# The end of a row-wise maximum kernel: who waits for the last store, and where the closing barriers stand

## The chip, the cores and the metric

The kernel runs on one core of one Trainium2 chip. The metric is the device time of one execution in microseconds (us), lower is better. Before the change it was 628.59 us (median of 3 runs, 628.57 to 628.78).

## The reference

```python
def setup_inputs():
    return {"x": np.random.randn(8192, 8192).astype(np.float32)}

def reference(x):
    return np.linalg.norm(x, ord=np.inf, axis=1)   # the largest |x| of each row
```

The kernel reads 268.44 MB and writes 8192 numbers.

## The kernel before

SyncE issues all loads, VectorE reduces each tile with an absolute maximum, and the results leave in three small stores. The last store, 128 numbers of four bytes, is issued by SyncE and waits for the last reduction.

```python
    for a in range(A):
        for n in range(G):
            t = sbuf.tile([P, W + PAD], F32, tag="t")          # three buffers
            nc.sync.dma_start(out=t[:, :W], in_=x_b[a, n])
            absmax(r_bulk[:, a, n * B : (n + 1) * B], ...)
    nc.scalar.dma_start(out=out_b, in_=r_bulk[:])
    # ... the last 16 rows of each partition in smaller and smaller loads ...
                    absmax(r_fin[:], t[:, lo : W + n_last - 1])  # the last reduction
    nc.sync.dma_start(out=out_t[:, n_tail - 1 :], in_=r_fin[:])  # the last store
    nc.at_finalize(start_first_load_early)                       # moves the first load ahead
```

Nothing in this source says how the program ends. The framework writes that: a last block of instructions in which, in this order,

1. SyncE waits for all eight DMA semaphores (100 to 107) and for VectorE's (99), in four two-semaphore waits and one drain;
2. all five engines meet in barrier one (each of the four others counts up semaphore 96, GpSimd waits for the four counts and then releases them through semaphore 97);
3. GpSimd drains and clears semaphores 99 to 107 with one range clear;
4. all five engines meet in barrier two, built like the first.

Of the kernel before, what the change touches and what calls it, by code (L numbers as in the profile page):

```python
# [1 line left out]
logging.getLogger("concourse").setLevel(logging.ERROR)  # L3

# [1 line left out]

# [4 lines left out]

F32 = mybir.dt.float32
X = mybir.AxisListType.X



TAIL = [
    [2944, 13440],
    [4096, 12288],
    [11520, 4864],  # L20
    [7680, 8704],
    [6528, 3328, 6528],
    [4864, 4096, 3328, 4096],
    [3968, 3584, 3328, 2944, 2560],
    [2432, 2176, 1920, 1664, 1536, 1280, 1152, 1024, 1152, 1024, 1024],
]


def segments(loads, cols):

    out, at = [], 0
    for i, w in enumerate(loads):
        end = at + w
        while at < end:
            r = at // cols
            to = min(end, (r + 1) * cols)
            out.append((i, r, at - r * cols, to - at))
            at = to
    return out


def start_first_load_early(nc):


    sp = mybir.EngineType.SP
    first, *rest = nc.main_func.blocks
    for block in rest:
        insts = block.instructions
        for i, ins in enumerate(insts):
            if ins.engine == sp and type(ins).__name__ == "InstDMACopy":  # L50
                assert not ins.sync_info.on_wait
                moved = insts[i]
                block.instructions = insts[:i] + insts[i + 1 :]
                head = first.instructions
                at = next(k for k, h in enumerate(head) if h.engine == sp)
                first.instructions = head[:at] + [moved] + head[at:]
                return


@with_exitstack  # L60
def kernel(
    ctx: ExitStack,
    tc: tile.TileContext,
    x: bass.AP,
    out: bass.AP,
    G: int = 4,
    B: int = 2,
    BUFS: int = 3,
    PAD: int = 16,
):  # L70
    nc = tc.nc
    P = nc.NUM_PARTITIONS
    rows, cols = x.shape
    W = B * cols


    n_tail = B * len(TAIL)
    n_bulk_rows = rows // P - n_tail
    assert n_bulk_rows % (G * B) == 0
    A = n_bulk_rows // (G * B)  # L80
    split = n_bulk_rows * P
    x_b = x[:split].rearrange("(a p n b) c -> a n p (b c)", p=P, a=A, n=G, b=B)
    out_b = out[:split].rearrange("(a p n b) -> p a (n b)", p=P, a=A, n=G, b=B)
    x_t = x[split:].rearrange("(p t b) c -> t p (b c)", p=P, b=B)
    out_t = out[split:].rearrange("(p t) -> p t", p=P)

    sbuf = ctx.enter_context(tc.tile_pool(name="sbuf", bufs=BUFS))
    outp = ctx.enter_context(tc.tile_pool(name="outp", bufs=1))

    segs = [segments(loads, cols) for loads in TAIL]  # L90
    count = {}
    for i, s in enumerate(segs):
        for _, r, _, _ in s:
            count[i * B + r] = count.get(i * B + r, 0) + 1
    n_last = count[n_tail - 1]
    k_max = max(count[r] for r in range(n_tail - 1))
    assert n_last - 1 <= PAD

    r_bulk = outp.tile([P, A, G * B], F32)
    r_tail = outp.tile([P, n_tail], F32)  # L100
    r_fin = outp.tile([P, 1], F32)
    part = outp.tile([P, n_tail - 1, k_max], F32)
    nc.vector.memset(part[:], 0.0)  # L103

    def absmax(o, i):
        nc.vector.reduce_max(out=o, in_=i, axis=X, apply_absolute_value=True)  # L106

    for a in range(A):
        for n in range(G):
            t = sbuf.tile([P, W + PAD], F32, tag="t")  # L110
            nc.sync.dma_start(out=t[:, :W], in_=x_b[a, n])
            absmax(
                r_bulk[:, a, n * B : (n + 1) * B],
                t[:, :W].rearrange("p (b c) -> p b c", b=B),
            )
    nc.scalar.dma_start(out=out_b, in_=r_bulk[:])

    seen = {}
    for i, loads in enumerate(TAIL):
        t = sbuf.tile([P, W + PAD], F32, tag="t")  # L120
        todo = segs[i]
        at = 0
        for j, w in enumerate(loads):
            nc.sync.dma_start(out=t[:, at : at + w], in_=x_t[i][:, at : at + w])  # L124
            at += w
            for _, b, c, n in [s for s in todo if s[0] == j]:
                r = i * B + b
                k = seen.get(r, 0)
                seen[r] = k + 1
                lo = b * cols + c  # L130
                if r < n_tail - 1:
                    absmax(part[:, r, k : k + 1], t[:, lo : lo + n])
                    if r == n_tail - 2 and k == count[r] - 1:

                        absmax(r_tail[:, : n_tail - 1], part[:])
                        nc.scalar.dma_start(
                            out=out_t[:, : n_tail - 1], in_=r_tail[:, : n_tail - 1]
                        )
                elif k < n_last - 1:
                    absmax(t[:, W + k : W + k + 1], t[:, lo : lo + n])  # L140
                else:

                    absmax(r_fin[:], t[:, lo : W + n_last - 1])
    nc.sync.dma_start(out=out_t[:, n_tail - 1 :], in_=r_fin[:])
    nc.at_finalize(start_first_load_early)


# [1 line left out]
_INS = ['x']  # L149
_OUTS = [((8192,), 'float32')]  # L150


# [23 lines left out]
```

## Time and profile before

The page of the profiled run before (span, busy share of the DMA engines in 40 slices, chain that ended last):

```profile
span 627.3 us, 201 instructions
...
DMA  9999999999999999999999999999999999999997
...
HBM read 268.44 MB, written 0.03 MB: 428 GB/s over the span
## 4 chain that ended last, share of the span: by engine, by line
DMA 67%; DVE 28%; another core or an unknown queue 4%; SPq 0%; issue 0%
```

The DMA engines are busy 90% or more in every slice but the last: the kernel is a read from memory at 428 GB/s. Nothing in the last block can change that; it can only change what happens after the reading. The timeline of the last two instructions (start, duration, engine, line, operation):

```profile
623.80 1.23 DVE L106 TENSOR_REDUCE r_fin<-t 128x1 f32<-128x1030 f32 x1
625.05 0.35 SPq L144 DMA_DIRECT2D out_dram<-r_fin  x1
```

The view of SyncE's waits (who waited for whom: total us, times, longest), and the DMA view's line of the last store (size of one, us from issue to landing):

```profile
SPq L171 <- DMA out_dram<-r_fin: 0.9, 1, 0.9
SPq L171 <- PEq L171: 0.6, 2, 0.4
```

```profile
out_dram<-r_fin SPq DMA_DIRECT2D x1, 0.5 KB, 1.4
```

L171 stands for the framework's last block. SyncE sits 0.9 us in an end wait for the last store, which takes 1.4 us to land; while it waits, the four other engines wait for it in barrier one. The view of one source line shows the block's instructions (count: duration in ns, least/median/most; first and last start):

```profile
L171 SPq EVENT_SEMAPHORE  x6: 17/28/898, 625.5 to 627.3; - x6
L171 POOLq EVENT_SEMAPHORE  x4: 17/17/17, 626.7 to 627.2; - x4
...
L171 POOLq EVENT_SEMAPHORE_RANGE_CLEAR  x1: 92/92/92, 626.9 to 626.9; - x1
```

SyncE has six semaphore instructions (four end waits, two in barriers), one of 898 ns; GpSimd's four belong to the two barriers and the first of them starts at 626.7, that is, after the landing.

The packed trace's own records of semaphores and instructions give this to the nanosecond (the views round to 0.1 us). Times are from the span's start:

```
625.024  VectorE   last reduction ends
625.052  SyncE     last store issued
625.587  SyncE     wait on semaphores 106 and 101, lasts 898 ns
626.463            sixteenth and last landing of the store on semaphore 101
626.485  SyncE     that wait ends
626.677  GpSimd    barrier one: all four counts seen
626.935  GpSimd    range clear, 92 ns
627.213  GpSimd    barrier two: release (17 ns), its last instruction
627.317  TensorE   out of barrier two: end of the span
627.552 627.586 627.791 627.835 627.858 627.957 627.996 628.030 628.077   semaphore 2 counted
628.863 ... 629.218                                                       counted nine times more
```

Semaphore 2 is not the kernel's. It belongs to what the runtime runs after the kernel, and that is inside the measured time: this run was timed at 629.09 us, and its last count of semaphore 2 is at 629.218.

### The profile page before, as it was taken

What the parts mean: (1) busy time and instruction counts of PE and PEld (TensorE: products, weight loads), DVE (VectorE), ACT (ScalarE), POOL (GpSimd) and SP (SyncE); (2) the same over time, 40 slices, a digit from 0 to 9 for tenths busy, and PEclk for the clock granted to TensorE, in tenths of its full rate; (3) what the DMA queues carried; (4) which work ended last, traced back from release to release, by engine and by line L of the source; (5) the groups of instructions that cost most, each with busy time, mean ns of one, the idle gap of its engine ahead of it and who ended that gap; (6) DMA issues with size and microseconds to landing.
All of it is one profiled execution on the core that took longest, in us unless ns stands there. A gap on an engine that the chain in (4) does not pass through costs nothing.

```text
span 627.3 us, 201 instructions
## 1 busy us (share of the span) xinstructions
DVE 553.0 (88%) x64; POOL 0.2 (0%) x4
## 2 busy tenths in 40 slices
DVE  0688998888988889888898888998889999999998
POOL 0000000000000000000000000000000000000000
DMA  9999999999999999999999999999999999999997
GB/s 401 468 401 468 401 468 401 464 405 455 414 451 418 451 418 401 468 401 468 401 468 401 468 401 468 401 468 401 468 418 406 460 430 410 436 422 430 428 423 287
DMA packets 8994, 268.49 MB, mean 428 GB/s; under 512 B 1952, under 2 KB 1952, under 8 KB 3104
## 3 DMA queue, kind: packets, MB, share of 16 engines
q1 hardware_dynamic: 8064, 268.44, 99.3%
q10 hardware_dynamic: 928, 0.03, 0.1%
q14 instruction: 2, 0.02, 0.0%
HBM read 268.44 MB, written 0.03 MB: 428 GB/s over the span
## 4 chain that ended last, share of the span: by engine, by line
DMA 67%; DVE 28%; another core or an unknown queue 4%; SPq 0%; issue 0%
DMA t<-in_x_dram 67%; DVE r_bulk L106 22%; DVE part L106 5%; DVE t L106 1%; DVE r_fin L106 0%; SPq L124 0%; DVE r_tail L106 0%
## 5 line engine op out<-in xcount | busy, mean ns | idle before, releaser
L106 DVE TENSOR_REDUCE r_bulk<-t 128x2 f32<-128x16384 f32 x24 | 413.3, 17220 | 70.1 <-DMA t<-in_x_dram 70.1
L106 DVE TENSOR_REDUCE part<-t 128x1 f32<-128x8192 f32 (+18 forms) x31 | 130.5, 4273 | 0.9 <-DMA t<-in_x_dram 0.6
L106 DVE TENSOR_REDUCE t<-t 128x1 f32<-128x1152 f32 (+3 forms) x6 | 7.9, 1387 | 0.0
L106 DVE TENSOR_REDUCE r_fin<-t 128x1 f32<-128x1030 f32 x1 | 1.2, 1226 | 0.0
L103 DVE MEMSET part<- 128x60 f32 x1 | 0.1, 108 | 0.9 <-PEq L160 0.9
L106 DVE TENSOR_REDUCE r_tail<-part 128x15 f32<-128x60 f32 x1 | 0.2, 216 | 0.0
L160 POOL MEMSET const-bfloat16-1.0<- 128x1 bf16 x1 | 0.1, 103 | 0.0
L160 POOL MEMSET const-uint8-127<- 128x1 uint8 x1 | 0.1, 103 | 0.0
L160 POOL MEMSET const-float32-1.0<- 128x1 f32 x1 | 0.1, 100 | 0.0
L160 POOL MEMSET const-float32-0.0<- 128x1 f32 x1 | 0.1, 99 | 0.2 <-issue 0.2
## 6 DMA issues: line engine op xcount, KB each, us to landing
t<-in_x_dram SPq DMA_DIRECT2D x1, 6720.0 KB, 40.4
t<-in_x_dram SPq DMA_DIRECT2D x2, 3264.0 KB, 26.4
t<-in_x_dram SPq DMA_DIRECT2D x3, 2048.0 KB, 29.0
t<-in_x_dram SPq DMA_DIRECT2D x1, 6144.0 KB, 40.6
t<-in_x_dram SPq DMA_DIRECT2D x1, 5760.0 KB, 35.3
t<-in_x_dram SPq DMA_DIRECT2D x3, 1664.0 KB, 32.5
t<-in_x_dram SPq DMA_DIRECT2D x2, 2432.0 KB, 32.6
t<-in_x_dram SPq DMA_DIRECT2D x1, 4352.0 KB, 42.8
```

The source lines that it names most:

```text
L103: nc.vector.memset(part[:], 0.0)
L106: nc.vector.reduce_max(out=o, in_=i, axis=X, apply_absolute_value=True)
L160: nc = _bacc.Bacc("TRN2", target_bir_lowering=False, num_devices=1)
```

## The change

The intent is that the closing barriers need not wait for the last store. After the change SyncE makes no end waits; the barriers start as soon as it has issued the store. GpSimd alone waits for all DMAs, behind both barriers, and then clears the semaphores. Since the program ends there, no engine should need a barrier behind the clear. That is argued.

```diff
+def finish_on_pool(nc):
+    sp, pool = mybir.EngineType.SP, mybir.EngineType.Pool
+    body, end = nc.main_func.blocks[-2:]
+    # ... finds the last store's semaphore (lane), SyncE's end wait (src),
+    # ... and GpSimd's drain and range clear (drain, clear) in the last block (insts) ...
+    waits = sorted(src.sync_info.on_wait, key=lambda s: s.id == lane)   # the last store's lane last
+    wait = mybir.InstDrain(
+        name=nc.get_next_instruction_name(),
+        engine=pool, ins=[], outs=[],
+        sync_info=mybir.SyncInfo(on_wait=waits, on_update=[]),
+    )
+    moved = {src.name, drain.name, clear.name}
+    end.instructions = [i for i in insts if i.name not in moved] + [wait, clear]
 ...
     nc.at_finalize(start_first_load_early)
+    nc.at_finalize(finish_on_pool)
```

More of the change, by code (lines that the diff above doesn't have):

```diff
@@ L57, in start_first_load_early @@
                 return
+def finish_on_pool(nc):
+    sp, pool = mybir.EngineType.SP, mybir.EngineType.Pool
+    body, end = nc.main_func.blocks[-2:]
+    last_store = [
+        i
+        for i in body.instructions
+        if i.engine == sp and type(i).__name__ == "InstDMACopy"
+    ][-1]
+    lane = last_store.sync_info.on_update[0].id
+    insts = end.instructions
+    src = next(i for i in insts if i.engine == sp)
+    assert type(src).__name__ == "InstDrain" and not src.sync_info.on_update
+    at = next(k for k, i in enumerate(insts) if type(i).__name__ == "InstISA")
+    drain, clear = insts[at - 1], insts[at]
+    assert drain.engine == clear.engine == pool
+    assert type(drain).__name__ == "InstDrain"
+    assert not (drain.sync_info and drain.sync_info.on_wait)
+    waits = sorted(src.sync_info.on_wait, key=lambda s: s.id == lane)
+    assert waits[-1].id == lane
+    wait = mybir.InstDrain(
+        name=nc.get_next_instruction_name(),
+        engine=pool,
+        ins=[],
+        outs=[],
+        sync_info=mybir.SyncInfo(on_wait=waits, on_update=[]),
+    )
+    moved = {src.name, drain.name, clear.name}
+    end.instructions = [i for i in insts if i.name not in moved] + [wait, clear]
 @with_exitstack
```

## The prediction

> **What bounds the kernel now.** A read of 268.44 MB: the page's DMA row is 9 in 39 of 40 slices, mean 428 GB/s, and the chain of waits is 67% DMA. The change touches none of that; every load, reduction and store keeps its order. It touches only what follows the last store, so I read the end of the span (timeline, and the trace's records of semaphores). Times are us from the span's start:
>
> - 625.02: the last reduction ends. 625.05 to 625.40: SyncE issues the last store.
> - 625.45: SyncE begins four end waits. The third, for the last store's lane, is held until 626.485; the sixteenth landing came at 626.463 (DMA view: 1.4 us from issue to landing).
> - 626.52 to 626.65: SyncE's fourth wait, its drain, its arrival at barrier one.
> - 626.68 to 626.86: barrier one. 626.84 to 627.03: GpSimd's drain and its range clear (92 ns). To 627.317: barrier two, end of the span.
>
> So 0.85 us follow the landing in series, and for 1.0 us before it the engines only wait.
>
> **What the change does.** Both barriers start when SyncE has issued the store, about 625.45, while it is in flight. Estimates from the steps above: barrier one 0.2 us, barrier two without the clear 0.3, so both are over near 626.0. Then GpSimd does three waits already satisfied, 78 ns each (its spacing of two semaphore instructions), to about 626.25: still before the landing, which I leave at 626.46. So the barriers are wholly hidden. Behind the landing remain: wake 22 ns, step to the drain 40, drain 34 to 70, step 30, clear 92: about 0.24 us instead of 0.85. The span should end at about 626.70, 0.61 us earlier; every engine but GpSimd is done near 626.0.
>
> **How much of it counts.** The time measured, 628.59, exceeds the span, 627.3: something after the kernel's instructions counts too. The Trainium skill, Runtime: NRT & Kernel Launch, "The ~15µs preamble/postamble breakdown", names a barrier and a reset of 51 semaphores per engine there. This trace agrees that they exist: semaphore 2 counts from 627.55 to 628.08, and nearly all others are reset by 628.64. In that barrier the third arrival is late: 205 ns after the second, against 38 ns at the same place in the barrier before the kernel. I take it for GpSimd, 0.56 us after its last instruction at 627.23. If it keeps that distance from its new last instruction (626.72), it arrives at 627.28, 0.51 us earlier, and the rest shifts with it. The gain is 0.5 to 0.6 us, nearly all on the critical path, but under 0.1% of the whole.
>
> **Predicted time: 628.05 us**, 628.59 less 0.54, range 627.7 to 628.4. Faster by over 2%: 0.5%; within 2%: 99%; slower by over 2%: 0.5%.
>
> **What would show each step right or wrong.** Both barriers' records between 625.4 and 626.1 on all engines; no end wait of SyncE; one long GpSimd wait ending some 20 ns after the last landing; drain and clear last, the clear ending at 626.65 to 626.75; landing still 1.4 us after issue; loads and reductions within 0.1 us of before; the semaphore-2 count resumed about 0.5 us earlier.
>
> **What would make it wrong.** The loads' time, 622 us, drifting by a few tenths between runs or chips, which could hide or double the gain. GpSimd's three satisfied waits running past the landing. The after-kernel part hanging on an engine other than GpSimd, or having a fixed wait of its own. The clear, now last, costing more than its record tells.

## The result, and the profile after

The changed kernel took 628.01 us (median of 6 runs, 627.88 to 628.20) against 628.63 us before in the same rounds (628.43 to 629.10). The two groups of runs do not overlap. The ratio, which is the mean time of the fast runs of one kernel over that of the other's of the same rounds and so not quite the ratio of the medians, is 0.9989 with a 95% interval of 0.9976 to 1.0002. By that interval alone the gain would not be certain; the trace has to decide. Of the experiments below, only runs 6, 9 and 10 have an interval wholly below 1, and at a threshold of 2% every kernel here counts as the same.

The page after:

```profile
span 626.0 us, 199 instructions
...
DMA  9999999999999999999999999999999999999997
...
HBM read 268.44 MB, written 0.03 MB: 429 GB/s over the span
## 4 chain that ended last, share of the span: by engine, by line
DMA 67%; DVE 29%; another core or an unknown queue 4%; SPq 0%; issue 0%
```

The bulk is the same. The timeline's last two lines after:

```profile
623.11 1.23 DVE L139 TENSOR_REDUCE r_fin<-t 128x1 f32<-128x1030 f32 x1
624.37 0.35 SPq L177 DMA_DIRECT2D out_dram<-r_fin  x1
```

Here is a trap. The span is 1.3 us shorter, but the last reduction already starts 0.69 us earlier (623.11 against 623.80), although the change does nothing before it. The profiled run before was among the slowest of its group (629.09 us), the one after the fastest of its own (627.88 us). So 0.68 us of the difference of the two profiles lies before the end of the last reduction, where no instruction was changed: I call it drift of the loads. From here on I count from the end of the last reduction, and call the time from there to the last count of semaphore 2 the **tail**. It is 4.194 us before and 3.662 us after: **0.532 us** is what the change gained.

The view of SyncE's waits after, the DMA view's line of the last store, and the views of the two source lines that the last block's instructions now carry:

```profile
SPq L205 <- PEq L205: 0.4, 2, 0.3
```

```profile
out_dram<-r_fin SPq DMA_DIRECT2D x1, 0.5 KB, 1.4
```

```profile
L205 POOLq EVENT_SEMAPHORE  x4: 17/17/17, 624.9 to 625.3; - x4
...
L205 SPq EVENT_SEMAPHORE  x2: 17/17/17, 625.0 to 625.4; - x2
...
L205 POOLq EVENT_SEMAPHORE_RANGE_CLEAR  x1: 92/92/92, 626.0 to 626.0; - x1
```

```profile
bacc.py:44 POOLq EVENT_SEMAPHORE  x4: 42/42/43, 625.4 to 625.8; - x4
```

SyncE's wait for the store is gone from its list. The four barrier instructions of GpSimd are at 624.9 to 625.3, before the landing (625.78), where they were behind it. The four new end waits are GpSimd's (the line of bacc.py:44). The store takes 1.4 us as before. In the trace's records, from the end of the last reduction:

```
                                         before    after
last store issued                         0.028    0.027
barrier two over on GpSimd                2.206    1.004
third satisfied end wait over               -      1.303
last landing of the store                 1.439    1.440
clear ends                                2.003    1.706
end of the span                           2.293    1.706
semaphore 2, 1st count                    2.528    1.326
             2nd count                    2.562    1.360
             3rd count                    2.767    2.233
             9th count                    3.053    2.518
            18th count (tail)             4.194    3.662
```

The first two counts come 1.2 us earlier, and then the count stands still for 0.87 us until the third. So the third engine in the runtime's barrier is the one that everybody waits for. That it is GpSimd, the engine that finishes last, is still an inference here; runs 6, 7, 9 and 11 test it.

### The profile page after: what moved, and what is told of

Read it like the earlier page. It is cut to its first block, busy times and chain, and to the rows that moved or that the text cites. A ratio compares the mean times of both kernels' runs of the same rounds, so it can differ in the third digit from the quotient of the medians.

```text
span 626.0 us, 199 instructions
## 1 busy us (share of the span) xinstructions
DVE 552.9 (88%) x64; POOL 0.2 (0%) x4
## 4 chain that ended last, share of the span: by engine, by line
DMA 67%; DVE 29%; another core or an unknown queue 4%; SPq 0%; issue 0%
DMA t<-in_x_dram 67%; DVE r_bulk L139 22%; DVE part L139 5%; DVE t L139 1%; DVE r_fin L139 0%; SPq L157 0%; DVE r_tail L139 0%
```

## The experiments

Every kernel gave the right output. Each is an edit of the end of `finish_on_pool` (`insts` is the framework's last block, `at` the place of the clear in it); runs 6, 7, 9, 10 and 11 also change the engine of the new wait. The diffs are against the changed kernel. Three chips were used (runs 1 to 4, 5 to 8, 9 to 11); the times of the kernel before are from the same rounds and chip. All tails are read from the one profiled run of each kernel.

One part of the tail can be checked in every run, because each run lists its time and its span (to 0.1 us), and time less span is what follows the kernel's last instruction. It is 1.73 to 1.83 us in the 27 runs of the kernel before, 1.78 to 1.88 in eleven runs of the changed kernel, 1.27 to 1.35 in the ten where SyncE finishes, 1.44 to 1.50 with ScalarE and 1.37 to 1.45 with VectorE. So that part does not hang on a single profile.

**The theory (A):** the two barriers and the barrier side of the clear ran in series behind the store's landing, and now run while it is in flight; what is left behind the landing is GpSimd's drain, its clear, and its way into the runtime's barrier. **Rivals:** the medians differ by drift of the loads (N); moving the waits off SyncE is what helps, wherever the barriers stand (B); the barriers still cost something (C); GpSimd is not what the end waits for (D).

### 1. The changed kernel again

No edit.

> The changed kernel once more, timed beside the kernel before on this chip. Tail means the time from the end of the last reduction to the last count of semaphore 2 in the trace: 4.19 us in the profile before, 3.66 after. Theory A (the barriers and the clear's barrier now run while the store is in flight): tail 3.66 again within 0.05, time 0.45 to 0.65 us under before. Rival N (the 0.62 us of the medians were mostly drift of the loads): tail may still be 3.66, but the two groups of times overlap, with medians under 0.3 us apart.

Measured: tail 3.652 us; 628.06 us (627.83 to 628.48) against 628.58 (628.45 to 629.06, 9 runs), 0.52 us under. The ranges now overlap by 0.03 us. This fits A, and N falls: the tail repeats within 0.01 us, and the gain of the medians agrees with that of the tail. (The interval of the ratio, 0.9978 to 1.0005, would not settle it.)

### 2. Only the waiter changes

```diff
-    end.instructions = [i for i in insts if i.name not in moved] + [wait, clear]
+    end.instructions = [wait] + [i for i in insts if i.name != src.name]
```

> Only the waiter changes: GpSimd makes the end waits ahead of barrier one instead of SyncE; drain and clear stay between the barriers. Theory A: nothing is hidden behind the store, so tail 4.1 to 4.3 us and time within 0.2 us of before. Rival B (the gain comes from taking the waits off SyncE): tail near 3.66, time 0.4 to 0.6 us under before.

Measured: tail 4.243 us; 628.66 us (628.51 to 629.02), 0.08 us over before. Giving the waits to GpSimd in the old place gains nothing, as A expected. B falls.

### 3. The waits and the clear between the barriers

```diff
+    gone = {src.name, drain.name, clear.name}
+    head = [i for i in insts[:at] if i.name not in gone]
+    tail = [i for i in insts[at:] if i.name not in gone]
-    end.instructions = [i for i in insts if i.name not in moved] + [wait, clear]
+    end.instructions = head + [wait, clear] + tail
```

> Barrier one runs while the store is in flight, then GpSimd waits and clears, then barrier two. Theory A: the barrier behind the clear is on the path again and barrier one is not; from the records, GpSimd's last instruction would end 0.20 us later after the clear than in the changed kernel, so tail 3.85 to 3.95 us, time 0.2 to 0.4 us under before. Rival (one barrier alone carries all of the gain): tail 3.66 or 4.19.

Measured: tail 3.893 us; 628.23 us (628.14 to 628.44), 0.35 us under before. Both halves of the change contribute: taking barrier one and its surroundings from behind the landing gained 4.194 - 3.893 = 0.301 us, taking barrier two as well another 3.893 - 3.662 = 0.231 us. GpSimd's last instruction ended 0.196 us later than in the changed kernel (1.902 against 1.706), where the records of before had led me to expect 0.20. The view of the last block shows the split: GpSimd's four barrier instructions stand at 625.1 (before the landing at 625.95) up to 626.4 (after it).

```profile
L208 POOLq EVENT_SEMAPHORE  x4: 17/17/17, 625.1 to 626.4; - x4
...
L208 POOLq EVENT_SEMAPHORE_RANGE_CLEAR  x1: 92/92/92, 626.1 to 626.1; - x1
```

### 4. No barriers at all

```diff
-    end.instructions = [i for i in insts if i.name not in moved] + [wait, clear]
+    end.instructions = [wait, clear]
```

> The changed kernel without the two closing barriers at all: GpSimd waits and clears, the others just end. Theory A says the barriers are wholly hidden: tail 3.66 within 0.04 us, time as the changed kernel's within 0.15 us. Rival C (they still cost something, by GpSimd being late for the landing or by the other engines' late end): tail shorter by 0.1 us or more.

Measured: tail 3.707 us; 628.03 us (627.96 to 628.40). GpSimd's clear ended at 1.712 us and its count came at 2.239, against 1.706 and 2.233 with both barriers: leaving them out gains nothing, so they are wholly hidden, and C falls. The tail is even 0.045 us longer, just outside what I wrote: the distance between the ninth and the tenth count is 0.825 us here and 0.788 in the changed kernel. The other kernel without barriers (run 10) has 0.829. Why that part of the runtime's work takes 0.04 us more there I did not find out.

### 5. Four empty drains on GpSimd ahead of its waits

```diff
-    end.instructions = [i for i in insts if i.name not in moved] + [wait, clear]
+    end.instructions = [i for i in insts if i.name not in moved] + [
+        mybir.InstDrain(name=nc.get_next_instruction_name(), engine=pool, ins=[], outs=[])
+        for _ in range(4)
+    ] + [wait, clear]
```

> The changed kernel with four empty drains on GpSimd between barrier two and its waits; a drain and its step took some 75 ns in the records, so 0.3 us more. In the profile after, GpSimd's third satisfied wait ended at 1.30 us after the last reduction and the landing came at 1.44, so with the step to the fourth wait it has about 0.09 us to spare. Theory A (the hidden time is bounded by the store's flight): the first 0.09 us cost nothing, tail 3.66 + 0.21 = 3.8 to 3.95 us. Rival D (GpSimd is not on the path, or has plenty to spare): tail 3.66. Rival E (nothing is hidden): 3.96 or more.

Measured: tail 3.796 us, 628.33 us (628.06 to 628.66) against 628.75; the tail is at the lower edge of what I wrote. The drains were cheaper than I had put them: from the release of barrier two to the first end wait 0.342 us passed where it had been 0.096, so 0.246 us for the four. The last end wait began 1.597 us after the last reduction instead of 1.464, 0.133 us late, and the tail grew by 0.134. So 0.246 - 0.133 = 0.113 us were swallowed and the rest was paid in full. D and E both fall, and this is the spare time of the changed kernel: 0.11 us. The two barriers are hidden; a third should show, since the releases of the two stand 0.33 us apart (0.659 and 0.987), but no run had three.

### 6. SyncE finishes

All of the change stays; only the engine of the waits and of the clear is another.

```diff
+    last = mybir.EngineType.SP
     ...
-        engine=pool,
+        engine=last,
     ...
+    nc.sync.sem_clear(range(99, 108))
+    # ... takes this clear of SyncE's (new_clear) out of the block where it was put ...
     ...
-    end.instructions = [i for i in insts if i.name not in moved] + [wait, clear]
+    end.instructions = [i for i in insts if i.name not in moved] + [wait, new_clear]
```

> All of the change is kept, but SyncE makes the waits and the clear behind the barriers instead of GpSimd. Theory G (the 0.53 us between the last instruction and the arrival in the barrier of the runtime belong to GpSimd; the tensor engine took 0.235): SyncE ends at about 1.66 us after the last reduction and arrives at 1.9 to 2.0 as the fifth, where the fifth count was 2.30; tail 3.25 to 3.4 us, time 0.2 to 0.4 us under the changed kernel. Rival F (whichever engine ends last needs the same 0.53 us): fifth count near 2.2, tail 3.5 to 3.6.

Measured: tail 3.059 us; 627.43 us (627.34 to 627.98) against 628.75 (628.44 to 628.95), ratio 0.9982, interval 0.9969 to 0.9996. The late count is now the fifth, at 1.751 us, 0.116 us after SyncE's last instruction; the third, no longer held up, comes 0.562 us after GpSimd's last one, as before the change (0.561). F falls. G was right in kind and too timid in size, its tail 0.19 us too long: SyncE needs 0.116 us, less than TensorE's 0.235, and its clear took 48 ns where GpSimd's took 92. The changed kernel was not timed in these rounds; against the kernel before, the median fell by 1.32 us, where the changed kernel's had fallen by 0.62 and 0.52.

### 7. ScalarE finishes

The same edit with ScalarE.

> As the run before, with ScalarE as the engine that waits and clears. ScalarE is taken for the second in the runtime's barrier. Theory G: it arrives some 0.25 us after its last instruction, at 1.9 to 2.0, then three more counts of about 0.1 us in all; tail 3.35 to 3.5 us. Rival F: arrival near 2.2, tail 3.6 to 3.7. If the order of the engines in that barrier is not as I take it, the count that comes late in the trace is not the second.

Measured: tail 3.240 us; 627.89 us (627.57 to 628.14) against 628.75. The late count is the second, at 1.771 us, 0.114 us after ScalarE's last instruction. Again shorter than I had expected; F falls here too, and ScalarE is placed second. The third count comes only 38 ns after the late second, at 1.809 us, though GpSimd had ended at 1.006 and would have been due at about 1.57: an engine's count waits for the one before it.

### 8. No clear

```diff
-    end.instructions = [i for i in insts if i.name not in moved] + [wait, clear]
+    end.instructions = [i for i in insts if i.name not in moved] + [wait]
```

> The changed kernel without the clear; GpSimd's waits are last. The trace shows the runtime resetting the same semaphores afterwards, so the output and a second execution should be right. Theory A: the clear is in series behind the landing, so the tail is shorter by its 92 ns and its step of 30 ns: 3.52 to 3.58 us. Rival H (the clear costs more than its record tells): tail 3.4 or less. Rival I (it is hidden in GpSimd's own ending): 3.66.

Measured: tail 3.774 us; 627.99 us (627.84 to 628.31) against 628.75. The tail misses all three expectations, because in this one profile the last store landed late: 1.674 us after the last reduction, where the other profiles have 1.432 to 1.443. Counted from the landing, the tail is 3.774 - 1.674 = 2.100 us, against 3.662 - 1.440 = 2.222 in the changed kernel: 0.122 us shorter, the clear's 92 ns and its step of 30. That fits A, but it is a reading after the fact and from one profile. (The third count comes 0.602 us after the last record here, not 0.53: that record is the last wait, and the drain behind it, which has no record, still runs.) The time cannot tell it from the changed kernel's. It is also a kernel that leans on the runtime resetting its semaphores, so I would not keep it.

### 9. SyncE finishes, again

> SyncE as the engine that waits and clears, once more, beside the next two. Theory G with the distances measured in the first run of it (0.116 us from SyncE's last instruction to its arrival in the runtime's barrier, 0.53 for GpSimd): tail 3.06 us within 0.05, time 0.9 to 1.4 us under before. If the first run was luck of the loads, the time comes back to 0.5 under before.

Measured: tail 3.053 us; 627.32 us (627.20 to 627.47) against 628.69 (628.34 to 628.95), ratio 0.9978, interval 0.9965 to 0.9992. It repeats. All ten runs of this kernel (of runs 6 and 9) are below all eighteen of the kernel before. The medians differ by 1.32 and 1.37 us; the tail accounts for 1.14 of it. The spans place the rest: in both comparisons the median span fell by 0.9 us, while the profiles have the span end only 0.66 and 0.67 us sooner after the last reduction, so some 0.2 us lie before it. Run 10, with the same finisher, does not have them (1.21 us of the medians, 1.19 of the tail), which fits drift of the loads; its cause is not shown. The views of its last block: SyncE now has the four end waits and the clear, and GpSimd's barrier instructions are over at 625.5, before the landing at 625.98.

```profile
bacc.py:44 SPq EVENT_SEMAPHORE  x4: 27/28/28, 625.7 to 626.0; - x4
```

```profile
L214 POOLq EVENT_SEMAPHORE  x4: 17/17/17, 625.1 to 625.5; - x4
```

```profile
L91 SPq EVENT_SEMAPHORE_RANGE_CLEAR  x1: 48/48/48, 626.1 to 626.1; - x1
```

### 10. SyncE finishes, without barriers and clear

```diff
-        engine=pool,
+        engine=sp,
-    end.instructions = [i for i in insts if i.name not in moved] + [wait, clear]
+    end.instructions = [wait]
```

> SyncE waits as in the run beside it; no closing barriers and no clear, as the trace shows the runtime resetting these semaphores afterwards. The barriers are hidden and give nothing; the clear and its step (0.10 us between the drain and the clear's end on SyncE) come off the series behind the landing. Theory G: the late count at 1.65 us after the last reduction, tail 2.93 to 3.03 us. If leaving out the barriers costs or gains by itself, the tail lies outside that.

Measured: tail 3.003 us; 627.48 us (627.26 to 628.09). The late count came at 1.653 us, 0.09 us earlier than in run 9, but 0.04 of it was given back between the ninth and tenth counts, as in run 4. The time cannot tell it from run 9. There is no reason to give up the clear for it.

### 11. VectorE finishes

> VectorE as the engine that waits and clears, behind the barriers. Taken for the fourth in the runtime's barrier: the fourth count comes late. Theory G (the long ending is GpSimd's own; SyncE and ScalarE took 0.12 us, the tensor engine 0.235): it arrives 0.1 to 0.25 us after its last instruction, at 1.77 to 1.95 after the last reduction, tail 3.1 to 3.3 us. Rival: any engine that computes has a long ending, arrival at 2.1 or later, tail 3.5 or more.

Measured: tail 3.239 us; 628.09 us (627.92 to 628.35) against 628.69. The late count is the fourth, at 1.851 us, 0.134 us after VectorE's last instruction. The rival falls: a computing engine need not have a long ending. The time is only 0.60 us under before where the tail says 0.96. The spans place the difference before the last reduction, as in run 9: the median span fell by 0.2 us only, where the profiles have it end 0.58 us sooner after the reduction, so the reading ended some 0.4 us later in these four runs.

### Together

"Last instruction" and "late count" are in us from the end of the last reduction; "distance" is the one less the other.

| finisher (run) | last instruction | late count | distance | tail |
|---|---|---|---|---|
| GpSimd, kernel before | 2.206 (barrier two) | 3rd, 2.767 | 0.561 | 4.194 |
| GpSimd, changed kernel | 1.706 (clear) | 3rd, 2.233 | 0.527 | 3.662 |
| SyncE (9) | 1.626 (clear) | 5th, 1.743 | 0.117 | 3.053 |
| ScalarE (7) | 1.657 (clear) | 2nd, 1.771 | 0.114 | 3.240 |
| VectorE (11) | 1.717 (clear) | 4th, 1.851 | 0.134 | 3.239 |

The distance is not all that counts. ScalarE's is as short as SyncE's, and yet its tail is 0.19 us longer, because it is counted second and the counts behind it have to follow: from the late count to the ninth it is 0.324 us for the second place (ScalarE), 0.285 for the third (GpSimd), 0.241 for the fourth (VectorE) and 0.163 for the fifth (SyncE). SyncE is the best finisher here on both scores. Of the 0.61 us that it gains on GpSimd, 0.49 come from the earlier late count and 0.12 from the shorter rest.

With the second to the fifth place taken, the first is left for TensorE; on that reading it counts 0.234 us after its last instruction in the changed kernel (1.092 to 1.326), where it waits for nobody. Why GpSimd's way out is so long the runs do not show.

## Why the prediction was right

- **The bound and the size.** Predicted 628.05 us, measured 628.01; predicted gain 0.54 us, measured 0.53 in the tail and 0.62 and 0.52 in the two comparisons of medians. Right, but that it is right to a few hundredths is partly luck: the six runs spread over 0.32 us, and 0.54 was a figure between the estimates for the span (0.61) and for the third count (0.51).
- **The barriers are hidden behind the store.** Right: barrier two was over on GpSimd at 1.004 us after the last reduction (predicted "near 626.0", which is 0.98), the records of both barriers lie between 0.43 and 1.09 us after it (predicted 0.38 to 1.08), and runs 2, 3 and 4 show that the place of the barriers, not the waiter, carries the gain.
- **The three satisfied waits on GpSimd.** Their cost was mis-sized: I took 78 ns for each from the spacing of its barrier instructions; the records start 91 and 87 ns apart. They ended at 1.303 instead of about 1.23, 0.14 us before the landing instead of 0.21. It did not matter: run 5 found 0.11 us still to spare.
- **0.24 us behind the landing instead of 0.85.** Measured 0.266 from the landing to the clear's end. Nearly right. Between the last wait and the clear, where the drain is (it has no record of its own), 0.108 us passed, within the 0.104 to 0.140 that I had allowed; what I had left out is the 42 ns of the last wait itself after its wake of 24 ns. The span's part of the gain was 0.587 us, predicted 0.61.
- **The late third count is GpSimd's.** I had only taken it to be so. Runs 6, 7, 9 and 11 show it: with another engine as the finisher, the late count is the fifth, the second or the fourth; and where nothing before it is late (runs 6, 9 and 11), the third comes 0.56 us after GpSimd's last instruction. The distance to it was not quite fixed: 0.527 us behind a clear, 0.561 behind a barrier's release, so the third count moved by 0.534 us where I had 0.51.
- **"Loads and reductions within 0.1 us of before."** Wrong: the profiled runs differ there by 0.68 us. The prediction named this drift as a danger, but expected the two profiles to agree, and the absolute "clear ending at 626.65 to 626.75" fell with it (626.05).
- **"One long GpSimd wait ending some 20 ns after the last landing."** Half right. The wait ended when the landing came, but the record is not long: it begins at 625.804, 24 ns after the landing at 625.780, and lasts 42 ns.
- **What it did not ask:** whether GpSimd was the right engine. The 0.56 us of GpSimd stood in the prediction as a constant to be carried along. It was the larger half of what there was to gain: 0.53 us from moving the barriers, another 0.61 from letting SyncE finish.

## What to carry to other kernels

Where a program ends with a small store, its flight (here 1.4 us) is time in which the closing barriers can run for nothing; put the wait for it behind them, and try which engine should do it: here the best one had a short way out and came last in the runtime's order. This is one kernel on one core, so measure it again elsewhere. Count the gain from an event that the change cannot move (here the end of the last reduction): across whole runs, drift of the loads was as large as the effect. Look at what is counted after the kernel's last instruction too; 0.47 of the 1.14 us that run 9 gained lay there, outside the span.

## What the Trainium skill lacked or had wrong

- Runtime: NRT & Kernel Launch, "The ~15µs preamble/postamble breakdown": it does not say that the engines leave the kernel at different speeds. From the last recorded instruction to the count in the runtime's barrier GpSimd took 0.53 to 0.56 us (0.60 in run 8, where an unrecorded drain came last), TensorE 0.234, VectorE 0.134, SyncE 0.116 and ScalarE 0.114. Nor does it give the order of that barrier, which the runs showed for four engines: ScalarE second, GpSimd third, VectorE fourth, SyncE fifth; the first place, left for TensorE, is an inference.
- The same section gives some 1.5 us for the barrier after the kernel and 1.5 us for the reset of semaphores. In the trace of before, the nine counts of that barrier took 0.53 us (627.552 to 628.077; 0.76 us from the end of the span), and the resets seen, which begin after its sixth count, took 0.66 us (627.976 to 628.638). Its 44 ns a hop agrees: the nine counts just before the kernel took 0.371 us, eight hops of 46 ns.
- Perfetto Trace Analysis, "Sequencer-only Instruction (DRAIN, etc)": it says that the recorded start is when all semaphores are satisfied, so that no wait is in the record. For an instruction that waits on two semaphores the trace shows otherwise: before, the wait on 106 and 101 has a record of 898 ns that ends 22 ns after 101's landing, since 106, named first, was satisfied long before. After, with the late semaphore named first, the record is 42 ns long and begins 24 ns after the landing; on SyncE too (run 9) it is then 28 ns long and begins 17 ns after. The record begins when the first-named semaphore is satisfied and holds the wait for the second. Run 4 has both ends in one wait of GpSimd, on 106 and then 103: semaphore 106 was complete 3.912 us before the end of the last reduction and the record begins 24 ns after that; 103 was complete 3.711 us before it, and the record, 207 ns long, ends 30 ns after that.
- DMA: Bandwidth & Descriptors, "Anatomy of one DMA — SWDGE (gpsimd) path": it puts a fixed cost of about 2 us on a DMA, most of it the receipt of the write; it is about the software path, and for a store issued by SyncE the page has a first-byte latency but no such split. The store of this kernel took 1.41 us: 0.84 from the issue to the first packet (625.052 to 625.896), 0.20 for the packets (to 626.095) and 0.37 from there to the last landing. Most of the time lay ahead of the packets, not behind them.
- No page has the cost of a semaphore range clear by engine. The records show 92 ns on GpSimd, 103 on VectorE, 81 on ScalarE and 48 on SyncE.
